# A hybrid decoder layer on one core: decay products and first-level operands of the HGRN2 heads computed in the gate projection

## The chip, the cores and the metric

The kernel runs on one core of one Trainium2 chip. The metric is the device time in microseconds of an execution; the time of a kernel is the median over its runs. Engines are named as in the profile: PE is TensorE, DVE is VectorE, ACT is ScalarE, POOL is GpSimd, SP is SyncE, whose queue issues nearly all loads and stores in program order.

## The reference, cut to what matters

One decoder layer on 1024 tokens with 16 meta tokens ahead of them: an HGRN2 recurrence with four heads beside a causal pooling branch, the two joined by sigmoid gates, then a gated MLP. The change lies in the recurrence and in what feeds it:

```
u = rmsnorm(h, mix_norm_pre[l])
proj = u @ w_in[l]
q, f_logit, i_in, g_out, v_pool, gate_a, gate_b = jnp.split(proj, cuts, axis=-1)
...
f = lb + (1.0 - lb) * jax.nn.sigmoid(fl)
k = (1.0 - lb) * jax.nn.sigmoid(-fl)
...
b = jnp.cumsum(lf, axis=2)
o_inter = jnp.einsum('bhtk,bhkv->bhtv', q * jnp.exp(b), state)
decay = jnp.where(causal, jnp.exp(jnp.where(causal, diff, 0.0)), 0.0)
scores = jnp.einsum('bhtk,bhtsk,bhsk->bhts', q, decay, k)
```

`lf` is the logarithm of `f`, `diff` the difference of two values of `b`. The score of a query at t and a key at s is thus the sum over 128 channels of q times k times the product of all f between s and t. The state carries the same products from chunk to chunk.

## The kernel before, in words

Values are float32, and every matmul operand is split into a high and a low part (`whi`, `wlo`; `uhi`, `ulo`), so that three passes make one product (L304, L305, L307 in the Strassen stages; L204, L205, L208 elsewhere). The stages follow one another: the normed input and the value projection, to about 85 us; the **Strassen pass**, 89.6 to 326 us; the **heads' stage**, 327 to about 584, in which the recurrence shares the engines with the pooling branch; then the mixer and the MLP.

The Strassen pass makes the projections for the forget logits (units F0, F1), the queries (Q0, Q1) and the branch gates (A0 to A3, B0 to B3), in the order F0, Q0, F1, Q1, A0 and on. A unit is 256 columns, that is two heads of F or Q, and takes seven products instead of eight. Each product accumulates in one of four PSUM pairs (`P`). Its weight operand is split four products ahead: ScalarE makes `whi` (L249), VectorE `wlo` (L250). Where the operand is a sum of weight blocks, GpSimd forms it first (`swa`, `swb`; L275 to L278) as soon as the raw weights (`wraw`) have landed. VectorE adds products up: L349 and L358 within a unit, and `put_gate` (L862, L864) for a finished part, which frees the PSUM pair. A part is one head and one half of the tokens.

For a part of an F unit `put_gate` calls `put_f`: ScalarE takes the sigmoids, VectorE scales and floors f (L635, L636), then divides k by f at odd positions for the smallest blocks (L647, L648), giving `kb`. f, k and kb are stored to DRAM (`fscr`, `kscr`, `kbscr`). A part of a Q unit is stored as it is (`qscr`). Temporary tiles come from one pool of 26 slots (`slot`), and a new tile waits until the last use of the slot it takes.

In the heads' stage `ORDER` is a string whose words say which step comes next in the program: `h0` to `h3` advance one head by one step, `PVa0` and the like are halves of the pooling projection (tile `ppv`), `G` the output gate (`pg`), `PP`, `BA`, `BB` the pooling and branch products (`pbb`), `sp` and `sa` elementwise steps, `w` weights for the next stage. Every engine works in its own program order, so an instruction behind a waiting one waits too.

`head_steps` loads f, q, kb and k of a head (L655 to L658), about 0.5 MB each. Causal scores are made in chunks of 128 tokens, by levels of block size 1 (the `sb` product, L719), 2, 4, 8, 16, 32 and 64 (the `sl` products, L696 and L690). At a level the keys of an even block have been multiplied by the f up to their block's end, the queries of an odd block by the f from its start. `grow(lv)` takes operands from one level to the next: keys L673 (`uk`), queries L679 (`uq`; at level 1 it is L677), and the block products of f themselves L681, in place in f. The words in `POOLED` go to GpSimd, among them `uk1` of all heads. Ahead of the `sb` product L714 multiplies the queries at odd positions by f. Scores go from PSUM to SBUF by masked copies (L711, L721) up to level 16 and by plain copies on VectorE at levels 32 and 64 (L705). After the last level k is transposed (`pt`, L748, L751), the states are made (`ds`, L765, with L768 taking the product of f over a chunk as decay), and the output (`po`, L785, L786) is normed by `ms` (L794 to L796) and gated.

## Time and profile before

| | us |
|---|---|
| median of three runs | 1337.79 |
| lowest, highest | 1334.33, 1338.15 |
| the profiled execution itself | 1336.16 |
| its span, first to last instruction | 1334.5 |
| PE busy | 1292.2 |
| DVE busy | 972.5 |
| ACT busy | 519.0 |
| POOL busy | 405.2 |

The granted TensorE clock is 0.988 on average over the span. How such a profile is read: times are microseconds from the first instruction; an engine's idle time is put down to what ended it; idle time of an engine that is not the bottleneck costs nothing. A row of a group gives line, engine, operation, tiles, shapes and count, then busy time, mean nanoseconds of one, and the idle time ahead of it. A row of a timeline gives start, duration, engine and line. A row of waits gives who waited for whom: total, times, longest.

### The profile page before, as it was taken

The numbers are of one execution on the slowest core, as the hardware profiler recorded it, in microseconds if no ns is written. First come the engines' busy times: TensorE is split into PE (matmuls) and PEld (weight loads), VectorE is DVE, ScalarE is ACT, GpSimd is POOL, SyncE is SP. The second block draws the span as 40 slices with busy tenths as digits, with TensorE's granted clock in tenths as the row PEclk, the third lists the DMA queues.
The fourth block names the chain that finished last, engine by engine and source line by source line (L and its number), as shares of the span: only waits on it lengthen the run. The fifth ranks groups of instructions, "written<-read, shape, count | busy, mean of one in ns | idle before, by whom it ended". The sixth has DMA issues, their size and how long they took to land.

```text
span 1334.5 us, 21944 instructions
## 1 busy us (share of the span) xinstructions
PE 1292.2 (97%) x8617; PEld 1143.3 (86%) x8617; DVE 972.5 (73%) x1287; ACT 519.0 (39%) x891; POOL 405.2 (30%) x325
## 2 busy tenths in 40 slices
PE   8999999999789879999999999999999999999997
PEld 6799899999788779987899888888888888888886
DVE  6768965542786976686668999888988885455757
ACT  5554433333125445224664222222222223454543
POOL 3015333322354100052026555446556652000000
PEclk9999999999899889999999999999999999999999
DMA  8135643334232276887686777776767799676644
GB/s 271 41 109 178 199 136 103 111 119 146 92 114 100 65 253 191 305 286 248 225 301 225 209 206 191 201 205 152 180 164 148 178 244 301 216 230 223 221 173 158
DMA packets 143802, 247.62 MB, mean 186 GB/s; under 512 B 11000, under 2 KB 75164, under 8 KB 143698
## 3 DMA queue, kind: packets, MB, share of 16 engines
q1 hardware_dynamic: 131634, 221.83, 49.4%
q0 software_dynamic: 12064, 24.38, 10.9%
q8 instruction: 68, 1.11, 0.3%
q14 instruction: 36, 0.29, 0.1%
HBM read 174.11 MB, written 95.09 MB: 202 GB/s over the span
## 4 chain that ended last, share of the span: by engine, by line
PE 62%; DVE 0%; issue 0%; ACT 0%; DMA 0%; DVEq 0%
PE P L305 11%; PE P L304 11%; PE P L307 11%; PE pd L184 5%; PE pd L185 5%; PE pd L186 5%; PE pm L184 2%; PE pm L185 2%; PE pm L186 2%; PE pba L204 1%; PE pba L205 1%; PE pba L208 1%; PE pbb L204 1%; PE pbb L205 1%; PE pbb L208 1%; PE pt L1271 1%
## 5 line engine op out<-in xcount | busy, mean ns | idle before, releaser
L305 PE MATMUL P<-v,whi 128*128 128x512 f32 (+2 forms) x408 | 140.7, 353 | 0.0
L304 PE MATMUL P<-v,whi 128*128 128x512 f32 (+2 forms) x408 | 140.7, 352 | 0.0
L307 PE MATMUL P<-v,wlo 128*128 128x512 f32 (+2 forms) x424 | 135.1, 349 | 0.0
L275 POOL TENSOR_TENSOR swa<-wraw,wraw 128x512 f32<-128x512 f32 x32 | 48.5, 1516 | 192.1 <-DMA wraw<-in_w_in_dram 98.7
L249 ACT CAST whi<-wraw 128x512 fp32r<-128x512 f32 x90 | 53.1, 618 | 102.3 <-PE P L305 75.7
L1511 DVE TENSOR_TENSOR rot<-wraw,rot 128x1024 fp32r<-128x1024 f32 x31 | 38.0, 1224 | 72.2 <-ACT rot L1510 72.2
L304 PEld LDWEIGHTS P<-v,whi 128*128 128x128 f32 x408 | 76.7, 188 | 10.4
L305 PEld LDWEIGHTS P<-v,whi 128*128 128x128 f32 x408 | 76.6, 188 | 10.2
L307 PEld LDWEIGHTS P<-v,wlo 128*128 128x128 f32 x424 | 74.1, 188 | 10.8
L185 PE MATMUL pd<-rot 128*128 128x512 f32 x272 | 82.1, 389 | 0.0
L186 PE MATMUL pd<-rot 128*128 128x512 f32 x272 | 82.1, 389 | 0.0
L184 PE MATMUL pd<-rot 128*128 128x512 f32 x272 | 81.1, 389 | 0.1
L250 DVE TENSOR_TENSOR wlo<-wraw,whi 128x512 fp32r<-128x512 f32 x86 | 77.4, 922 | 2.7 <-ACT whi L249 2.7
L250 DVE TENSOR_TENSOR wlo<-swb,whi 128x512 fp32r<-128x512 f32 x64 | 67.6, 1064 | 9.7 <-ACT whi L249 9.6
L249 ACT CAST whi<-swa 128x512 fp32r<-128x512 f32 x64 | 38.1, 618 | 92.6 <-PE P L305 77.4
L304 PE MATMUL P<-uhi,whi 128*128 128x258 f32 (+2 forms) x240 | 68.6, 303 | 0.0
L305 PE MATMUL P<-ulo,whi 128*128 128x258 f32 (+2 forms) x240 | 68.4, 303 | 0.0
L1510 ACT CAST rot<-wraw 128x1024 fp32r<-128x1024 f32 x31 | 32.7, 1054 | 90.7 <-PE pd L186 89.4
L249 ACT CAST whi<-swb 128x512 fp32r<-128x512 f32 x64 | 38.1, 618 | 70.9 <-PE P L305 61.5
L304 PE MATMUL P<-t2h,whi 128*128 128x258 f32 (+2 forms) x228 | 65.2, 304 | 0.3 <-DVE sg L864 0.3
L304 PE MATMUL P<-t4h,whi 128*128 128x258 f32 (+2 forms) x228 | 65.5, 304 | 0.0
L305 PE MATMUL P<-t4l,whi 128*128 128x258 f32 (+2 forms) x228 | 65.3, 304 | 0.0
(383 smaller groups left out, 3884.9 us busy)
## 6 DMA issues: line engine op xcount, KB each, us to landing
wraw<-in_w_in_dram SPq DMA_DIRECT2D x36, 512.0 KB, 4.8
yt<-ysum SPq DMA_DIRECT2D x33, 512.0 KB, 5.4
wraw<-in_ffn_w_gate_dram SPq DMA_DIRECT2D x26, 512.0 KB, 5.9
wraw<-in_ffn_w_up_dram SPq DMA_DIRECT2D x22, 512.0 KB, 6.5
wsum<-in_ffn_w_down_dram SPq DMA_DIRECT2D x22, 512.0 KB, 8.5
wraw<-in_w_out_dram SPq DMA_DIRECT2D x18, 512.0 KB, 5.1
ysum<-ys SPq DMA_DIRECT2D x11, 768.0 KB, 5.6
sa<-sscr SPq DMA_DIRECT2D x16, 513.0 KB, 4.4
```

Source lines behind the costliest of these rows:

```text
L184: pe.matmul(ps, ahi, bhi, start=first, stop=False)
L185: pe.matmul(ps, ahi, blo, start=False, stop=False)
L186: pe.matmul(ps, alo, bhi, start=False, stop=last)
L204: pe.matmul(ps[:, :n], whi[:, k, :], xhi, start=(k == 0), stop=False)
L249: act.copy(hi, src)
L250: (pool_e if 4 <= i < 2 * self.early else dve).tensor_tensor(lo, src, rr(hi), ALU.subtract)
L275: pool_e.tensor_tensor(s1, a21, a22, ALU.add)
L304: pe.matmul(d, whi[:, k, :], xh[:, c : c + w], start=(k == 0 and onto is None), stop=False, **go)
L305: pe.matmul(d, whi[:, k, :], xl[:, c : c + w], start=False, stop=False, **go)
L307: pe.matmul(x[:, o : o + w], wlo[:, k, :], xh[:, c : c + w], start=False, stop=(k == 3), **go)
L1510: act.copy(hi, src)
L1511: dve.tensor_tensor(lo, src, rr(hi), ALU.subtract)
```

## The change

In `put_f` the arithmetic of the forget gate's first level is added: the keys at even positions times the next f (`grow(1)` for keys, now L658) and all products of f over blocks of 2, 4, up to 128 tokens (L667, seven instructions, each made from the one before). They lie behind the part in its own tile, widened to 2 x HX, and are stored to a new tensor `tscr`; the store of k comes after the even positions are changed. The halves of a head are stored separately, each with 32 columns of halo, made by ScalarE copies and GpSimd memsets. `put_q` is new: it loads f of the same head and half back from `fscr`, makes the queries for the `sb` product (L678) and for level 2 (L680), and stores both (`qbscr`, `qscr`).

`head_steps` loads five tensors, qb, kb, q, k and tot (L690 to L694). `grow` keeps the key and query products alone (now L717), one line over both halves of the tokens, reading the totals from `tot`; L714, L677 and L681 have no successor in the heads' stage, and `uk1` leaves `POOLED`. A head has one step fewer, and `ORDER` is written anew. The loads of heads 0 and 1 are to be issued after the pass's last weight load (`gates.loaded`) rather than after the last load of any stage so far. The copies of levels 32 and 64 go to ScalarE (L739).

VectorE's program order at the first F part of the pass, before; `sg` is the part being made (later kb), `fk` holds f and k:

```order
L647 RECIPROCAL sg_1102<-fk_1104 128x256
L648 TENSOR_TENSOR sg_1102<-sg_1102,fk_1104 128x256
L862 TENSOR_TENSOR sg_1145<-p_154_1014,P_164_1118 128x514
L250 TENSOR_TENSOR wlo_1185<-swa_1153,whi_1184 128x512 x2
L250 TENSOR_TENSOR wlo_1243<-swb_1154,whi_1242 128x512
L862 TENSOR_TENSOR sg_1246<-p_166_1148,P_175_1217 128x528
```

The same place now:

```order
L656 TENSOR_TENSOR sg_1104<-sg_1104,fk_1106 128x256
L658 TENSOR_TENSOR fk_1106<-fk_1106 128x272
L667 TENSOR_TENSOR sg_1104<-fk_1106 128x272
L667 TENSOR_TENSOR sg_1104<-sg_1104 128x136
L667 TENSOR_TENSOR sg_1104<-sg_1104 128x68
L667 TENSOR_TENSOR sg_1104<-sg_1104 128x34
L667 TENSOR_TENSOR sg_1104<-sg_1104 128x16
L667 TENSOR_TENSOR sg_1104<-sg_1104 128x8
L667 TENSOR_TENSOR sg_1104<-sg_1104 128x4
L891 TENSOR_TENSOR sg_1158<-p_154_1016,P_164_1131 128x514
L678 TENSOR_TENSOR sg_1158<-sg_1158,fq_1160 128x256
L680 TENSOR_TENSOR sg_1158<-sg_1158,fq_1160 128x512
```

Eight instructions of the F part stand between its last one and the next `put_gate` (L862, now L891), and two of the Q part, which read `fq` loaded back from DRAM, ahead of the next `wlo`. Later in the pass the totals of several parts stand mixed with one another and with the adds.

SP's program order at the end of the pass, before:

```order
L147 DMA wraw_3857<-in_w_in_dram 128x8x128
L871 DMA sscr<-sg_3340 128x512
L655 DMA f_3395<-fscr 128x1056
L656 DMA q_3398<-qscr 128x1026
L657 DMA kb_3397<-kbscr 128x1024
L871 DMA sscr<-sg_3369 128x514
L658 DMA k_3396<-kscr 128x1056
```

And now:

```order
L147 DMA wraw_3978<-in_w_in_dram 128x8x128
L898 DMA sscr<-sg_3474 128x512
L690 DMA qb_3530<-qbscr 128x1024
L691 DMA kb_3529<-kbscr 128x1024
L692 DMA q_3532<-qscr 128x1026
L898 DMA sscr<-sg_3503 128x514
L693 DMA k_3531<-kscr 128x1088
L694 DMA tot_3533<-tscr 128x2x538
L690 DMA qb_3542<-qbscr 128x1024
L691 DMA kb_3541<-kbscr 128x1024
```

The first load of head 0 stands behind the same weight load and the same store (`sscr`, the gates of the branches) in both; what is loaded, and in which order, differs.

VectorE's program order at the start of the heads' stage, before; `near` collects the scores of small blocks:

```order
L714 TENSOR_TENSOR q_3398<-q_3398,f_3395 128x512
L677 TENSOR_TENSOR q_3398<-q_3398,f_3395 128x1024
L721 COPY_PREDICATED near_3457<-mbase,sb_3462 128x256
L714 TENSOR_TENSOR q_3408<-q_3408,f_3405 128x512
L681 TENSOR_TENSOR f_3395<-f_3395 128x528
L677 TENSOR_TENSOR q_3408<-q_3408,f_3405 128x1024
L721 COPY_PREDICATED near_3502<-mbase,sb_3507 128x256
L673 TENSOR_TENSOR k_3396<-k_3396,f_3395 128x264x2
L679 TENSOR_TENSOR q_3398<-q_3398,f_3395 128x256x2
```

And now:

```order
L751 COPY_PREDICATED near_3593<-mbase,sb_3597 128x256
L717 TENSOR_TENSOR k_3531<-k_3531,tot_3533 128x272x2
L717 TENSOR_TENSOR q_3532<-q_3532,tot_3533 128x256x2
L745 COPY_PREDICATED near_3593<-mask_145,sl_3631 128x64x2
L751 COPY_PREDICATED near_3716<-mbase,sb_3720 128x256
L745 COPY_PREDICATED near_3716<-mask_145,sl_3754 128x64x2
L717 TENSOR_TENSOR k_3543<-k_3543,tot_3545 128x272x2
```

The five instructions on q and f ahead of the first growth of k are gone. On PE the order is now 42 pooling matmuls, `sb` of head 0, 16 more, its first `sl`, 14 more, then `sb` and the first `sl` of head 1.

The diff, cut to its core:

```diff
@@ -53,10 +53,10 @@
-ORDER = ("h0 h1 PVa0 h0 h1 PVb0 h0 h1 h0 PVa1 h1 h0 sp0 PVb1 h1 h0 h1 PVa2 sp1 h0 h1 PVb2 h0 h1 h2 h0 PVa3 sp2 h1 h0 h1 h3 "
...
+ORDER = ("h0 h1 PVa0 h0 PVb0 h1 h0 PVa1 h1 h0 sp0 PVb1 h1 h0 PVa2 h1 h0 sp1 PVb2 h1 h0 h2 PVa3 h1 h0 sp2 h3 PVb3 h1 h0 h2 Ga2 sp3 h1 h0 h3 h2 "
...
-POOLED = ("uk1.0 uk1.1 uk1.2 uk1.3 wBA2 wBA6 wBA7 wBB2 wPP2 wPV0 wPV1 wPV2 wPV3 wG2 wG3 "
+POOLED = ("wBA2 wBA6 wBA7 wBB2 wPP2 wPV0 wPV1 wPV2 wPV3 wG2 wG3 "
...
@@ -589,6 +589,13 @@
+    HX = M0 + HN
+
+    TOTALS, at_ = {}, 0
+    for lv in (2, 4, 8, 16, 32, 64, 128):
+        TOTALS[lv] = at_
+        at_ += (HX if lv <= NM else HN) // lv
+    NTOT = at_
...
@@ -625,75 +629,105 @@
-    def put_f(m, half, g):
-
-        n = HN if half else HF
-        both = slot(2 * HP, name="fk")
-        f, k = both[:, :n], both[:, HP : HP + n]
-        act.activation(f, g, AF.Sigmoid)
-        act.activation(k, g, AF.Sigmoid, scale=-1.0)
-        dve.tensor_scalar(f, f, oml[:, m : m + 1], lb[:, m : m + 1], ALU.mult, ALU.add)
-        dve.tensor_scalar(f, f, LOG_FLOOR, None, ALU.max)
-        act.activation(k, k, AF.Copy, scale=oml[:, m : m + 1])
-        t0 = NM + (HF if half else 0)
-        for t, d in ((f, fdr), (k, kdr)):
-            nc.sync.dma_start(d[m][:, t0 : t0 + n], t)
-            if not half:
-                nc.sync.dma_start(d[m][:, :NM], t[:, :NM])
-        f2, k2 = (t[:, n - HN :].rearrange("p (b two) -> p b two", two=2) for t in (f, k))
+    def twos(t):
+        return t.rearrange("p (b two) -> p b two", two=2)
+
+    def put_f(m, half, whole, n):
+
+        g, tot = whole[:, :n], whole[:, HX : HX + NTOT]
+        both = slot(2 * HX, name="fk")
+        f, k = both[:, :HX], both[:, HX:]
+        act.activation(f[:, HX - n :], g, AF.Sigmoid)
+        act.activation(k[:, HX - n :], g, AF.Sigmoid, scale=-1.0)
+        dve.tensor_scalar(f[:, HX - n :], f[:, HX - n :], oml[:, m : m + 1], lb[:, m : m + 1], ALU.mult, ALU.add)
+        dve.tensor_scalar(f[:, HX - n :], f[:, HX - n :], LOG_FLOOR, None, ALU.max)
+        act.activation(k[:, HX - n :], k[:, HX - n :], AF.Copy, scale=oml[:, m : m + 1])
+        if half:
+            pool_e.memset(f[:, :M0], 1.0)
+            pool_e.memset(k[:, :M0], 0.0)
+        else:
+            for t, last in ((f, 1.0), (k, 0.0)):
+                act.copy(t[:, :NM], t[:, NM:M0])
+                pool_e.memset(t[:, NM - 1 : NM], last)
+        nc.sync.dma_start(fdr[m][:, half], f[:, M0:])
         kb = g[:, n - HN :]
-        b2 = kb.rearrange("p (b two) -> p b two", two=2)
-        act.copy(b2[:, :, 0], k2[:, :, 0])
-        dve.reciprocal(b2[:, :, 1], f2[:, :, 1])
-        dve.tensor_tensor(b2[:, :, 1], b2[:, :, 1], k2[:, :, 1], ALU.mult)
+        act.copy(twos(kb)[:, :, 0], twos(k[:, M0:])[:, :, 0])
+        dve.reciprocal(twos(kb)[:, :, 1], twos(f[:, M0:])[:, :, 1])
+        dve.tensor_tensor(twos(kb)[:, :, 1], twos(kb)[:, :, 1], twos(k[:, M0:])[:, :, 1], ALU.mult)
         nc.sync.dma_start(kbdr[m][:, half * HN : half * HN + HN], kb)
+        dve.tensor_tensor(twos(k)[:, :, 0], twos(k)[:, :, 0], twos(f)[:, :, 1], ALU.mult)
+        nc.sync.dma_start(kdr[m][:, half], k)
+        src = f
+        for lv in TOTALS:
+            if lv == 2 * NM:
+                src = src[:, M0 // NM :]
+            src = twos(src)
+            w = src.shape[1]
+            dst = tot[:, TOTALS[lv] : TOTALS[lv] + w]
+            dve.tensor_tensor(dst, src[:, :, 0], src[:, :, 1], ALU.mult)
+            src = dst
+        nc.sync.dma_start(tdr[m][:, half], tot)
+
+    def put_q(m, half, whole, n):
+
+        f = slot(HN, name="fq")
+        nc.sync.dma_start(f, fdr[m][:, half])
+        q, q1 = whole[:, n - HN : n], whole[:, HX : HX + HN]
+        if not half:
+            nc.sync.dma_start(qdr[m][:, :HALO], whole[:, :HALO])
+        dve.tensor_tensor(twos(q)[:, :, 1], twos(q)[:, :, 1], twos(f)[:, :, 1], ALU.mult)
+        nc.sync.dma_start(qbdr[m][:, half * HN : half * HN + HN], q)
+        dve.tensor_tensor(twos(q1), twos(q), twos(f)[:, :, :1].to_broadcast([P, HN // 2, 2]), ALU.mult)
+        nc.sync.dma_start(qdr[m][:, HALO + half * HN : HALO + half * HN + HN], q1)
 
     def head_steps(h):
-        f, k, kb, q = slot(NM + L, name="f"), slot(NM + L, name="k"), slot(NM + L, name="kb"), slot(NM + L, name="q")
+        kb, qb, k, qm, tot = (slot(n, name=w) for w, n in (("kb", SEQ), ("qb", SEQ), ("k", 2 * HX), ("q", TQ),
+                                                           ("tot", 2 * HX)))
+        q = qm[:, HALO:]
+        tot = tot.rearrange("p (s t) -> p s t", s=2)[:, :, :NTOT]
         vmeta = small([NM, P], "vmeta", "vmeta", 2)
-        with tc.issue_after(stage["load"].ins):
-            nc.sync.dma_start(f, fdr[h])
-            nc.sync.dma_start(q[:, NM + T0 :], qdr[h])
-            nc.sync.dma_start(kb[:, M0:], kbdr[h])
-            nc.sync.dma_start(k, kdr[h])
+        with tc.issue_after((stage["load"] if h >= 2 else gates.loaded).ins):
+            nc.sync.dma_start(qb, qbdr[h])
+            nc.sync.dma_start(kb, kbdr[h])
+            nc.sync.dma_start(qm, qdr[h])
+            nc.sync.dma_start(k.rearrange("p (s t) -> p s t", s=2), kdr[h])
+            nc.sync.dma_start(tot, tdr[h])
             nc.sync.dma_start(vmeta, vmd[:, h * P : (h + 1) * P])
         yield
-        pool_e.memset(f[:, NM - 1 : NM], 1.0)
-        pool_e.memset(k[:, NM - 1 : NM], 0.0)
         sc, near = slot(NCH * P, name="sc"), small([P, NCH * SB], "near", "near", 2)
         n3 = near.rearrange("p (c t) -> p c t", c=NCH)
         scm = small([NM, HALO], "scm", "scm", 2)
         pool_e.memset(near, 0.0)
         pool_e.memset(sc, 0.0)
 
+        def own(c):
+            t = (c // 4) * HX + M0 + (c % 4) * P
+            return k[:, t : t + P]
+
         def grow(lv):
-            lo = 0 if lv < NM else M0
-            kc, fc, qc, fq_ = blocks(k, lo, lv), blocks(f, lo, lv), blocks(q, M0, lv), blocks(f, M0, lv)
-            n, nq = (NM + L - lo) // (2 * lv), SEQ // (2 * lv)
-            eng(f"uk{lv}.{h}").tensor_tensor(kc[:, :, 0, :], kc[:, :, 0, :], fc[:, :, 1, :1].to_broadcast([P, n, lv]),
-                                             ALU.mult)
-            if lv == 1:
-                q2 = q[:, M0:].rearrange("p (b two) -> p b two", two=2)
-                dve.tensor_tensor(q2, q2, fq_[:, :, 0, :].to_broadcast([P, nq, 2]), ALU.mult)
-            else:
-                eng(f"uq{lv}.{h}").tensor_tensor(qc[:, :, 1, :], qc[:, :, 1, :],
-                                                 fq_[:, :, 0, :1].to_broadcast([P, nq, lv]), ALU.mult)
-            dve.tensor_tensor(fc[:, :, 0, :1], fc[:, :, 0, :1], fc[:, :, 1, :1], ALU.mult)
+            e = M0 if lv >= NM else 0
+            ks = k.rearrange("p (s t) -> p s t", s=2)[:, :, e:]
+            ks = ks.rearrange("p s (b two h) -> p s b two h", two=2, h=lv)[:, :, :, 0]
+            qs = q.rearrange("p (s b two h) -> p s b two h", s=2, two=2, h=lv)[:, :, :, 1]
+            t0, w = TOTALS[lv], (HX if lv <= NM else HN) // lv
+            x = w - HN // lv
+            tk, tq = (tot[:, :, t0 + o : t0 + w].rearrange("p s (b two) -> p s b two", two=2)
+                      for o in (x if e else 0, x))
+            for t, f in ((ks, tk[:, :, :, 1:]), (qs, tq[:, :, :, :1])):
+                dve.tensor_tensor(t, t, f.to_broadcast(list(t.shape)), ALU.mult)
 
...
                     n = 2 * lv * i
-                    dve.tensor_copy(o3[n : n + lv, :, n + lv : n + 2 * lv], p3[n : n + lv])
+                    act.copy(o3[n : n + lv, :, n + lv : n + 2 * lv], p3[n : n + lv])
                 return
...
-        q2, f2 = (t[:, M0:].rearrange("p (b two) -> p b two", two=2) for t in (q, f))
-        dve.tensor_tensor(q2[:, :, 1], q2[:, :, 1], f2[:, :, 1], ALU.mult)
         ps = bank("sb")
-        for c in range(NCH):
-            for n in range(0, P, SB):
-                own = slice(M0 + c * P + n, M0 + c * P + n + SB)
-                pe.matmul(ps[n : n + SB, c * SB : (c + 1) * SB], kb[:, own], q[:, own], start=True, stop=True)
-        grow(1)
+        for t in range(0, SEQ, SB):
+            c, n = t // P, t % P
+            pe.matmul(ps[n : n + SB, c * SB : (c + 1) * SB], kb[:, t : t + SB], qb[:, t : t + SB], start=True, stop=True)
         dve.copy_predicated(n3, mbase.rearrange("p (o t) -> p o t", o=1).to_broadcast([P, NCH, SB]),
                             ps[:, : NCH * SB].rearrange("p (c t) -> p c t", c=NCH))
-        yield
...
@@ -858,17 +885,17 @@
         kind, j = GUNITS[u]
         m, n = 2 * j + i, ghalo(u) + HN
         at = slice(n, n + HN) if h else slice(0, n)
-        g = slot(at.stop - at.start, name="sg")
+        whole = slot(2 * HX, name="sg")
+        n = at.stop - at.start
+        g = whole[:, :n]
         dve.tensor_tensor(g, a, b, ALU.add)
         if c is not None:
             dve.tensor_tensor(g, g, c, ALU.add)
-        if kind == "F":
-            put_f(m, h, g)
+        if kind in "FQ":
+            (put_f if kind == "F" else put_q)(m, h, whole, n)
             return
-        if kind != "Q":
-            act.activation(g, g, AF.Sigmoid)
-        to = dict(Q=qdr, A=sd, B=sd)[kind]
-        nc.sync.dma_start(to[m + (KD if kind == "B" else 0), :, at], g)
+        act.activation(g, g, AF.Sigmoid)
+        nc.sync.dma_start(sd[m + (KD if kind == "B" else 0), :, at], g)

```

37 lines of the change are left out of this document (16 added, 21 removed).

## The prediction

> **What bounds the kernel now.** I read the busy shares first, then the table of stretches (start:end, length, then each engine's busy time, at the end granted TensorE clock, DMA share, GB/s), then whom TensorE waits for.
>
> ```profile
> PE 1292.2 (97%) x8617; PEld 1143.3 (86%) x8617; DVE 972.5 (73%) x1287; ACT 519.0 (39%) x891; POOL 405.2 (30%) x325
> ```
> ```profile
> 120.00:150.00 30.00, 29.74 (x176) 26.24 (x175) 29.69 (x39) 12.32 (x23) 11.73 (x8) 1.00 0.59 190
> 150.00:180.00 30.00, 30.00 (x201) 27.68 (x200) 26.91 (x35) 12.82 (x24) 11.91 (x8) 1.00 0.54 172
> 180.00:210.00 30.00, 30.00 (x197) 27.53 (x196) 16.91 (x24) 11.30 (x20) 11.41 (x8) 1.00 0.35 119
> ...
> 326.00:340.00 14.00, 12.72 (x137) 12.10 (x136) 2.98 (x4) 2.13 (x3) 5.94 (x7) 1.00 0.98 350
> 340.00:360.00 20.00, 13.13 (x425) 12.67 (x426) 17.91 (x22) 2.52 (x5) 6.64 (x4) 0.74 0.07 21
> 360.00:380.00 20.00, 17.22 (x340) 16.56 (x339) 14.86 (x22) 6.55 (x15) 8.09 (x5) 0.91 0.10 29
> ...
> 420.00:440.00 20.00, 13.25 (x315) 12.36 (x314) 15.89 (x15) 14.04 (x18) 6.02 (x4) 0.89 0.10 29
> 440.00:460.00 20.00, 19.59 (x445) 18.14 (x445) 17.12 (x37) 6.02 (x14) 1.37 (x1) 0.94 0.19 55
> 460.00:480.00 20.00, 12.76 (x141) 11.83 (x130) 18.83 (x37) 11.37 (x26) 0.00 (x0) 0.83 0.68 210
> ```
>
> TensorE is the bound over the whole span. The change touches two stages. In the Strassen pass TensorE never rests, but from 120 to 180 VectorE is just as full (29.69 of 30): it is a second bound, hidden only because it keeps pace. In the heads' stage TensorE does rest, and these are its waits there, 326 to 510:
>
> ```profile
> PE sl L696 <- DVE q L677: 5.5, 1, 5.5
> PE ds L765 <- DMA vh<-vscr: 4.2, 1, 4.2
> PE sl L696 <- DVE q L679: 4.0, 4, 2.6
> PE sb L719 <- DVE q L714: 3.7, 1, 3.7
> PE sl L696 <- issue: 3.0, 1, 3.0
> PE po L785 <- ACT rs L796: 2.9, 1, 2.9
> PE pt L748 <- DVE k L673: 1.5, 1, 1.5
> PE pt L751 <- DVE plo L843: 1.5, 1, 1.5
> PE sl L690 <- DVE q L679: 1.4, 1, 1.4
> PE ppv L204 <- DVE sg L862: 0.9, 1, 0.9
> ```
>
> These are 28.6 us, most of it VectorE. A second loss is in the clock column: busy time times the missing clock is 13.13 x 0.26 + 17.22 x 0.09 + 13.25 x 0.11 + 19.59 x 0.06 + 12.76 x 0.17 = 9.8 us. So the stage loses some 38 us, the pass nothing; the change takes VectorE work out of the first and puts it into the second.
>
> **The pass: what is added.** Per forget-gate call (eight): the level-one k product L658 (128x272) and seven totals L667 (272 down to 4 wide). Per query call (eight): L678 (128x256) and L680 (128x512). Ahead of the first add of unit A0 stand 8, 51, 7 and 7 of these. Nearest rows, of today's program:
>
> ```profile
> 165.57 0.42 DVE L648 TENSOR_TENSOR sg<-sg,fk 128x256 f32<-128x256 f32 x1
> ```
> ```profile
> L648 DVE TENSOR_TENSOR sg<-sg,fk 128x256 f32<-128x256 f32 x8 | 7.8, 981 | 0.1
> ```
> ```profile
> L681 DVE TENSOR_TENSOR f<-f 128x132 f32<-128x132 f32 x4 | 1.7, 426 | 0.0
> L681 DVE TENSOR_TENSOR f<-f 128x66 f32<-128x66 f32 x4 | 1.1, 269 | 0.0
> L681 DVE TENSOR_TENSOR f<-f 128x32 f32<-128x32 f32 x4 | 0.9, 213 | 0.0
> L681 DVE TENSOR_TENSOR f<-f 128x16 f32<-128x16 f32 x4 | 0.7, 186 | 0.1
> L681 DVE TENSOR_TENSOR f<-f 128x8 f32<-128x8 f32 x4 | 0.6, 167 | 0.0
> ```
> ```profile
> 375.26 0.68 DVE L679 TENSOR_TENSOR q<-q,f 128x512 f32<-128x512 f32 x1
> ```
>
> L658 and L678 are priced as the undisturbed L648, 0.42; L680 as the undisturbed L679, 0.68. One call's totals: 0.42 + 0.43 + 0.27 + 0.21 + 0.19 + 0.17 + 0.17 = 1.86, times eight, less five late ones (0.9): 14.0. Sum: 8 x 0.42 + 14.0 + 7 x (0.42 + 0.68) = 25.1 us of VectorE. If each of the widest instructions takes the mean of L648, 0.98, instead, it is 8 x 0.98 + 8 x (0.98 + 1.44) - 0.9 + 7 x (0.98 + 0.98) = 40.0. How much is absorbed?
>
> ```profile
> 108.20 1.84 DVE L250 TENSOR_TENSOR wlo<-swa,whi 128x512 fp32r<-128x512 f32 x2 [3.74 <-ACT whi L249]
> ...
> 175.40 0.69 DVE L862 TENSOR_TENSOR sg<-p,P 128x514 f32<-128x514 f32 x1
> 176.01 1.29 DVE L250 TENSOR_TENSOR wlo<-wraw,whi 128x512 fp32r<-128x512 f32 x2
> 178.17 0.69 DVE L349 TENSOR_TENSOR p<-p,P 128x514 f32<-128x514 f32 x1 [0.88 <-PE P L307]
> 180.89 0.69 DVE L862 TENSOR_TENSOR sg<-p,P 128x512 f32<-128x512 f32 x1 [2.03 <-PE P L307]
> ```
>
> VectorE idles 3.7 us before 108.20, which the first totals can fill, and from there to 178 hardly at all. At 178.17 it waits for TensorE again: the 175.40 add is where it has caught up. Products end 2.72 us apart (180.89 - 178.17), and each has one of four PSUM pairs, so an add may come three products late, less its own 0.69, before TensorE stands: 7.5 us. What is left delays TensorE: 25.1 - 3.7 - 7.5 = 13.9, I take **+14**. After that VectorE has 13 us of 30 free (180 to 210) and catches up; TensorE, at 30.00 of 30, does not, so the delay stays. Bounds: +8 if two more products count as slack, since weights are split four products ahead (13.9 - 5.4); +29 from the sum of 40.0 (40.0 - 3.7 - 7.5). I stay by the undisturbed rows, since GpSimd is busy for only 23.6 of these 60 us and today's instructions have already taken their share of that.
>
> That contention is a row of its own:
>
> ```profile
> 128.10 1.78 DVE L250 TENSOR_TENSOR wlo<-wraw,whi 128x512 fp32r<-128x512 f32 x1
> ```
> ```profile
> 127.58 1.74 POOL L276 TENSOR_TENSOR swa<-swa,wraw 128x512 f32<-128x512 f32 x1
> ```
>
> This shape takes 1.78 beside GpSimd's weight sums, and 1.29 for two of it at 176.01, alone. The Trainium skill, GPSIMD Engine Reference, section 1. Specifications, has the rule: GpSimd shares its SBUF interfaces with VectorE, and instructions with two SBUF inputs contend. The trace agrees; all that is added reads two SBUF operands, and were all of it stretched, the sum would be the +29 above: the first rival.
>
> Also added: stores and loads by SP (the totals, the q copies, f read back). DMA is 0.59 busy there; but SP issues in order and GpSimd's sums wait for the weights behind those stores. Priced at nothing while weights arrive early; at 5 if a weight load is late.
>
> **The heads' stage: what goes.** L714, L677 and all L681 leave VectorE, the level-one k product leaves GpSimd, the twelve copies of L705 go to ScalarE, which is at most 14 of 20 busy. What opens in place of the waits at the start, by the landing of loads:
>
> ```profile
> 334.35 0.69 DVE L714 TENSOR_TENSOR q<-q,f 128x512 f32<-128x512 f32 x1 [7.54 <-DMA q<-qscr]
> ...
> 340.63 2.76 DVE L714 TENSOR_TENSOR q<-q,f 128x512 f32<-128x512 f32 x1 [2.60 <-DMA q<-qscr]
> ```
> ```profile
> 327.35 0.32 PE L204 MATMUL ppv<-uhi,whi 128*128 128x346 f32 x1
> 327.51 0.32 PE L205 MATMUL ppv<-ulo,whi 128*128 128x346 f32 x1
> ...
> 343.44 1.08 PE L719 MATMUL sb<-q,kb 128*32 128x32 f32 x64 [3.68 <-DVE q L714]
> ```
>
> The second load landed at 334.3, the sixth at 340.6: 1.6 us each. SP's order keeps head 0's loads behind the same store as before, so "behind its weights" brings nothing here. There are now five loads a head. Head 0's first product needs loads 1 and 2 (334.3), head 1's needs 6 and 7 (342.2), its level one needs load 9 (345.4). Walking the new order from 327.0 (42 pooling matmuls, head 0's first product, 16, its level one, 14, head 1's first product, its level one; 0.16 us a pooling matmul by 327.51 - 327.35, 1.08 a block of head products, as at 343.44), TensorE waits 0.6, 0.9 and 2.1 us: 3.6. Gone from the waits above: 5.5, 4.0, 3.7, 3.0, 1.5 and 1.4, together 19.1. Staying: 4.2 (vh), 2.9, 1.5, 0.9. New waits later, where plo and level products now share VectorE with head 2's growth: 0 to 4, I take 1.5. So the waits change by -19.1 + 3.6 + 1.5 = -14.0; bounds -8 (half of the L679 and k waits remain under GpSimd's adds, 4 new) and -18. The clock, at its worst after the waits of 3.7 and 5.5 that go, gives 6 of 9.8 back (2 to 8): **-20** together, -10 to -26.
>
> A rule for the clock: the Trainium skill, TensorE: Matmul & The Clock Gate, Part 1, section What's actually happening, says an idle window of about 3.4 us halves the clock. By it only the vh wait still costs (12.76 x 0.17 = 2.2) and 7.6 come back, 1.6 more than I take; but 360 to 380 shows 0.91 where the longest wait was 2.6, so not by that alone.
>
> **Sum.** 14 - 20 = -6 against the execution's own 1336.16 (span 1334.5 and 1.66 around it), which lies 1.63 under the median 1337.79. Median: 1337.8 - 6 = about 1331.
>
> **Rivals.** (1) *VectorE cannot carry the pass* (slower): the added instructions are stretched by GpSimd's sums. For: VectorE is at 29.69 of 30, and L648's mean is 0.98. Against: GpSimd has 12 of 30 us. Price +29, gain -20: 1347. It decides once the add of 175.40 comes more than 20 us late by TensorE's clock of products, as the gain is 20. The Trainium skill's rule on shared interfaces speaks for it. Chance 0.2. (2) *A wait takes the place of the removed ones*: the loads of head 1 to 3, five each, or plo become late, so the waits give 8 and the clock 4, for the pass's 14: 1340. For: the DMA share is 0.98 already from 326 to 340; against: from 340 to 380 it is at most 0.10. Chance 0.18. (3) *The pass absorbs it*: both at their good ends, +8 and -26: 1320. For: the order puts adds between the small totals; against: the idle time of 3.7 us is all there is. Chance 0.2.
>
> **How the numbers follow.** Forecast 0.42 (1325 to 1337), rivals 0.2, 0.18, 0.2. A measurement of this kernel tells 0.3%, 4 us, from no change. Faster: 0.34 of the forecast and rival 3: 0.54. Within: 0.08 and most of rival 2: 0.24. Slower: rival 1 and the rest of 2: 0.22. The range takes in most of rivals 1 and 3: 1314 to 1348.
>
> **What would show it.** The last Strassen product ends 8 to 20 us later than 326; VectorE is near 30 of 30 from 110 to past 195, and TensorE's new waits fall between 130 and 200, on sg, p or wlo. Heads: 326 to 510 shrinks by about 20, TensorE waits there fall to about 14, and none names the q products of level one. I am wrong if the pass ends where it did, if it is over 20 late, or if waits on qb, kb, k or tot loads exceed 6 us.

## The result, and the profile after

The changed kernel takes 1342.78 us (median of 7 runs, 1340.48 to 1347.53); the kernel before, measured along with it, 1336.47 (7 runs, 1334.33 to 1338.15). The ratio is 1.0052, 95% interval 1.0036 to 1.0068: slower by half a per cent, 6.3 us. The forecast was 1331, faster; the range, 1314 to 1348, held the time. One execution, the profiled one of run e9 below, ran at a mean clock of 0.654 and took 1821.2 us; its trace is not read.

The profiled execution took 1343.94 us, span 1342.2, so 7.8 over the one shown of before. I place these 7.8 first, by three marks: the first pooling product (`ppv`), where the Strassen pass has ended, the first product of `pm`, where the heads' stage has ended, and the end. The tile views of ppv and pm, of before and of the changed kernel (line, engine, operation, count, shortest/median/longest ns, first and last start, shapes):

```profile
L204 PE MATMUL ppv<-uhi,whi x96: 316/323/657, 327.0 to 401.6; 128*128 128x346 f32 x64, 128*128 128x348 f32 x32
```
```profile
L184 PE MATMUL pm<-whi,zc x128: 389/389/500, 586.7 to 686.0; 128*128 128x512 f32 x128
```
```profile
L204 PE MATMUL ppv<-uhi,whi x96: 317/323/657, 343.3 to 408.5; 128*128 128x346 f32 x64, 128*128 128x348 f32 x32
```
```profile
L184 PE MATMUL pm<-whi,zc x128: 389/389/501, 594.4 to 693.8; 128*128 128x512 f32 x128
```

The pass ends 16.3 us later (343.3 - 327.0; forecast 14). The heads' stage shrinks from 259.7 (586.7 - 327.0) to 251.1 (594.4 - 343.3), by 8.6 where 20 were forecast. The rest, 747.8 in both spans (1334.5 - 586.7, 1342.2 - 594.4), is unchanged. So 16.3 - 8.6 = 7.7, which is the whole difference of the spans.

**The pass.** The table of stretches of the changed kernel, columns as in the prediction:

```profile
120.00:150.00 30.00, 22.62 (x132) 19.48 (x130) 29.44 (x51) 12.57 (x24) 11.25 (x14) 0.99 0.53 179
150.00:180.00 30.00, 27.77 (x143) 24.42 (x144) 27.25 (x53) 10.23 (x20) 11.63 (x13) 0.90 0.60 194
```

VectorE was at 29.69 in the first row before and could not get fuller: it has 51 instructions now instead of 39, and TensorE drops from 29.74 to 22.62. TensorE's waits from 90 to 340 (who, for whom: total, times, longest):

```profile
PE P L304 <- DVE sg L893: 6.9, 2, 6.1
PE P L304 <- DVE sg L891: 2.6, 3, 1.1
PE P L307 <- DVE wlo L250: 1.6, 1, 1.6
PE P L304 <- DVE p L358: 1.2, 1, 1.2
```

These are 12.3 us, all on VectorE (one of 0.3 on ScalarE's `whi` comes to them); before there was one wait of 0.3 in the pass. The second row above also has a clock of 0.90: 27.77 x 0.10 = 2.8 us, which the prediction did not price. It lies at the longest wait, which ends here (timeline of TensorE: start, duration, idle before it):

```profile
150.65 0.57 PE L304 MATMUL P<-t2h,whi 128*128 128x272 f32 x1 [6.11 <-DVE sg L893]
```

From 149.29, inside this wait, the clock is at half for 6.83 us, so the products behind it run slowly too.

**The heads' stage.** TensorE's waits of the changed kernel, 342 to 515:

```profile
PE sl L730 <- issue: 3.8, 2, 3.1
PE ms L821 <- ACT rh L862: 2.8, 1, 2.8
PE sl L730 <- DMA k<-kscr: 1.8, 1, 1.8
PE pt L779 <- ACT sc L739: 1.7, 1, 1.7
PE pt L776 <- DVE plo L870: 1.4, 1, 1.4
PE sl L725 <- DVE q L717: 1.0, 1, 1.0
PE sb L750 <- DMA kb<-kbscr: 1.0, 2, 0.6
```

With three more of 0.9 and one of 0.2 these are 16.4; before, the same list came to 29.8. So the waits fell by 13.4; the forecast was 14.0. The reader is to see that the longest single wait is now 3.1, where 5.5, 4.2 and 3.7 stood before. And yet the clock did not come back:

```profile
340.00:360.00 20.00, 16.75 (x285) 15.51 (x283) 4.23 (x8) 4.31 (x7) 5.61 (x4) 1.00 0.89 319
360.00:380.00 20.00, 18.88 (x463) 18.25 (x464) 9.39 (x16) 3.17 (x6) 3.97 (x4) 0.83 0.04 12
...
420.00:440.00 20.00, 16.90 (x292) 16.32 (x291) 10.82 (x23) 6.80 (x12) 6.57 (x4) 0.90 0.19 56
440.00:460.00 20.00, 15.26 (x319) 13.87 (x319) 11.14 (x20) 16.25 (x26) 1.56 (x1) 0.76 0.27 81
460.00:480.00 20.00, 20.00 (x253) 18.75 (x252) 12.70 (x18) 11.89 (x25) 0.00 (x0) 0.92 0.09 27
480.00:510.00 30.00, 26.92 (x177) 25.80 (x177) 22.00 (x44) 12.72 (x28) 0.00 (x0) 0.94 0.82 263
```

By the prediction's formula: 18.88 x 0.17 + 16.90 x 0.10 + 15.26 x 0.24 + 20.00 x 0.08 + 26.92 x 0.06 = 11.8 us, against 9.8 before. The stage's 8.6 are then -13.4 of waits, +2.0 of clock, +1.3 of a new wait at its end (`pm` for ScalarE's `zc`, at 593.2) and +1.5 that these rows don't assign.

**What the clock follows.** Half clock comes in pieces of 3.41, 6.83 or 10.24 us, one, two or three times 3.41. In the heads' stage of the changed kernel they start at 360.92, 436.01, 453.08 and 483.80 and last 6.83, 6.83, 10.24 and 3.41. That is 27.3 us, and it was 27.3 us before as well (10.24, 3.41, 6.83 and 6.83, from 343.33, 370.64, 435.50 and 473.04). What changed is how much of it TensorE was busy: 19.6 us before, 25.2 now. A busy microsecond at half clock loses half, so the loss goes from 9.8 to 12.6. Taken by these pieces the clock is +2.8 and not +2.0; with a wait of 0.5 behind 515 that leaves 0.2 of the 1.5 unassigned.

The starts, too, lie whole multiples of 3.41 apart (75.09, 17.07 and 30.72 are 22, 5 and 9 of them). So the clock looks set on a fixed grid of windows of 3.41 us. These are the windows right ahead of the four pieces:

```profile
357.51:360.92 3.41, 1.23 (x120) 1.15 (x123) 0.44 (x1) 1.36 (x4) 3.02 (x2) 1.00 0.73 273
432.60:436.01 3.41, 0.48 (x57) 0.39 (x47) 1.90 (x4) 3.16 (x5) 1.18 (x1) 1.00 0.57 167
449.67:453.08 3.41, 0.58 (x2) 0.30 (x2) 2.22 (x2) 3.40 (x7) 1.04 (x1) 1.00 0.00 0
480.39:483.80 3.41, 0.66 (x5) 0.42 (x6) 3.41 (x7) 3.41 (x9) 0.00 (x0) 1.00 0.43 96
```

TensorE was busy for 0.48 to 1.23 of 3.41 us in them, but none is idle throughout. In the last one the waits of 1.4 and 1.7 on `pt` from the list above stand one behind the other. In the first, TensorE issued 120 matmul instructions, more than in the twice as long piece behind it (111); but they are small, 32 wide by 32 or 16 columns, and the longest wait among them is 1.8 us. The theory that the runs below test: half clock follows a window of about 3.4 us in which the array did little, **whether it waited or had small products**. Its rival: only the time counts in which TensorE waited, added up over the window. The Trainium skill, TensorE: Matmul & The Clock Gate, Part 1, section What's actually happening, ties half clock to an idle window of about 3.4 us; the lengths agree (3.41 and its multiples), while here a window in which TensorE was busy for 1.23 of 3.41 us counted as idle.

### The profile page after: what moved, and what is told of

It reads as the page before. It is cut to its first block, busy times and chain, and to the rows that moved or that the text cites. A ratio compares the mean times of both kernels' runs of the same rounds, so it can differ in the third digit from the quotient of the medians.

```text
span 1342.2 us, 22057 instructions
## 1 busy us (share of the span) xinstructions
PE 1299.6 (97%) x8617; PEld 1147.9 (86%) x8617; DVE 969.0 (72%) x1319; ACT 525.2 (39%) x911; POOL 397.4 (30%) x329
## 4 chain that ended last, share of the span: by engine, by line
PE 55%; DVE 0%; ACT 0%; DVEq 0%; issue 0%
PE P L305 11%; PE P L304 11%; PE P L307 11%; PE pd L184 5%; PE pd L186 5%; PE pd L185 5%; PE pm L184 2%; PE pm L186 2%; PE pm L185 2%; PE pt L1298 1%; PE pm L1353 1%; DVE hrow L1708 0%; ACT junk L1695 0%; DVE acc L1771 0%; DVE p L1474 0%; DVEq L1799 0%
## 5 line engine op out<-in xcount | busy, mean ns | idle before, releaser
L275 POOL TENSOR_TENSOR swa<-wraw,wraw 128x512 f32<-128x512 f32 x32 | 53.3, 1665 | 170.6 <-DMA wraw<-in_ffn_w_gate_dram 72.0
L305 PEld LDWEIGHTS P<-v,whi 128*128 128x128 f32 x408 | 76.6, 188 | 10.2
L250 DVE TENSOR_TENSOR wlo<-wraw,whi 128x512 fp32r<-128x512 f32 x86 | 73.6, 877 | 2.7 <-ACT whi L249 2.7
L250 DVE TENSOR_TENSOR wlo<-swb,whi 128x512 fp32r<-128x512 f32 x64 | 64.1, 1008 | 8.4 <-ACT whi L249 8.4
L305 PE MATMUL P<-t2l,whi 128*128 128x258 f32 (+2 forms) x228 | 66.2, 308 | 0.0
```

The source lines that it names most:

```text
L250: (pool_e if 4 <= i < 2 * self.early else dve).tensor_tensor(lo, src, rr(hi), ALU.subtract)
L275: pool_e.tensor_tensor(s1, a21, a22, ALU.add)
L305: pe.matmul(d, whi[:, k, :], xl[:, c : c + w], start=False, stop=False, **go)
```

## The experiments

My theory of the pass: VectorE's added instructions among the F and Q units are the whole delay. The rival: the new stores and loads on SP make weights late. My theory of the heads: the clock, as above. Rivals: ScalarE's moved copies, and that clock is lost only where TensorE waits anyway. Line numbers are those of each kernel. All ratios are to the kernel before, run on the same chip. Differences from the changed kernel are of medians from different chips; by the ratios they come out up to 2 us larger or smaller.

**1 and 2. The added VectorE work moved behind A0.** Kernel e1_late_fq stores f, k and q raw, and does the level-one products and totals one task per store in units A0 to A3, from tiles loaded back; e2_late_f does so for the F part alone.

```diff
+        nc.sync.dma_start(krd[m][:, half], k)
...
+        late.append(lambda: late_f(m, half))
+
+    late = []
+
+    def late_f(m, half):
...
+        nc.sync.dma_start(f, fdr[m][:, half])
+        nc.sync.dma_start(k, krd[m][:, half])
         dve.tensor_tensor(twos(k)[:, :, 0], twos(k)[:, :, 0], twos(f)[:, :, 1], ALU.mult)
...
+        nc.sync.dma_start(qrd[m][:, half], whole[:, n - HN : n])
+        late.append(lambda: late_q(m, half))
...
         act.activation(g, g, AF.Sigmoid)
+        if late:
+            late.pop(0)()
```

> All added VectorE work (L658, the totals, the two query products) is taken out of the F and Q units: f, k and q are stored raw, loaded back and worked on in the puts of units A0 to B1, where VectorE has some 14 us of 30 free. Theory (VectorE's load in the F/Q units delays the pass by 16.3 us, the clock eats the heads' gain): the last Strassen product ends within 4 us of 326, the heads keep their 10 us, so about 1328, 8 us below the kernel before. Rival (the delay comes from SP's longer queue and slot waits, not from VectorE): more loads and stores make it no better, pass end 338 or later, 1339 or more.

> Only the F part is put off (L658 and totals, about 17 of 25 us); the query products stay in the Q units with their load of f. Theory by VectorE's load: 25.1 less 17.4 leaves 7.7, under the 11.2 that can be absorbed: pass end within 4 us of 326, about 1329. Rival (the query part, which waits for f from DRAM in the middle of VectorE's queue, is what costs): pass end 334 or later, 1335 or more.

Measured: e1 1335.40, ratio 0.9986 (0.9973 to 0.9998); e2 1335.87, 0.9987 (0.9977 to 0.9998). Both are faster than the changed kernel by some 7 us and hardly faster than before. Unit A0's products start at 169.25 before, at 184.20 in the changed kernel (+15.0), at 170.02 in e1 (+0.8) and at 172.84 in e2 (+3.6). So F's part made 11.4 of the 15 and Q's 2.8, and VectorE's added work there, with its waits for `fq`, is the cause; e1 has more stores and loads than the changed kernel, and with them the weights came in time, which speaks against SP's queue as the cause of this delay. But the pass of e1 still ends at 338.8, 11.9 late, where the theory had 4 at most, and that of e2 at 337.9. VectorE's waits in e1, 180 to 300:

```profile
DVE ql L695 <- DMA ql<-qrscr: 8.4, 5, 3.0
DVE tl L679 <- DMA fl<-fscr: 6.8, 4, 2.6
DVE ql L695 <- issue: 4.0, 1, 4.0
```

VectorE stood 19.2 us at the late tasks, 15.2 of it for tiles that were not back yet, with the adds that free PSUM queued behind; TensorE waited 9.5 us for VectorE from 170 on. The work, moved to where VectorE had room, brought the stall of its loads with it. So only 4.5 of e1's gain over the changed kernel lie in the pass. Another 5.9 lie in the heads' stage (245.2, 584.0 - 338.8), whose code is the same: there half clock came to 17.1 us instead of 27.3.

**5. The same with the loads two stores earlier.** Kernel e5_late_pre issues each task's loads two stores ahead of its work. It also spreads the tasks over 24 stores instead of 16.

```diff
+        if begun and begun[0][0] <= puts[0] - 2:
+            begun.pop(0)[1]()
+        if late and puts[0] % 3:
+            begun.append((puts[0], late.pop(0)()))
```

> As the version with all added VectorE work put off to units A and B, but each task's loads are issued two puts ahead of its arithmetic and the tasks are spread over 24 puts instead of 16. There TensorE lost 9.6 us in units A1 to A3 while VectorE stood 21 us waiting for the loads of f, k and q. Theory (VectorE has the time, the late loads cost it): pass end within 4 us of 326, about 1327. Rival (SP's queue, full of weight loads and stores, makes loads late however early they are asked for): pass end 334 or later, 1334 or more.

Measured: 1334.62, ratio 0.9977 (0.9965 to 0.9989). The pass ends at 335.9, 8.9 late. VectorE's waits, 180 to 338:

```profile
DVE ql L708 <- DMA ql<-qrscr: 13.2, 5, 4.7
DVE fl L680 <- DMA fl<-krscr: 9.3, 4, 3.0
```

22.5 us still, and pass end and time are where the rival on this run had them. SP issues in order, and its queue stood for 35.6 us, from 170 to 335, at the gates' stores (L929), which waited for ScalarE's `sg`; an earlier place in the program does not pass what stands ahead. The loads on another queue were not tried.

**3. The copies back on VectorE.** Kernel e3_copies_dve undoes this one part.

```diff
-                    act.copy(o3[n : n + lv, :, n + lv : n + 2 * lv], p3[n : n + lv])
+                    dve.tensor_copy(o3[n : n + lv, :, n + lv : n + 2 * lv], p3[n : n + lv])
```

> The changed kernel with the copies of levels 32 and 64 back on VectorE. Theory: they are off the chain, 1343 give or take 2. Rival (ScalarE's later releases make the waits of 1.7 and 3.1 us that TensorE now has on ScalarE in the heads' stage): 3 or more us faster, 1339 or less.

Measured: 1339.76, ratio 1.0026 (1.0012 to 1.0039): some 3 us under the changed kernel by the medians, though the two intervals touch. That is between the theory (1341 to 1345) and its rival (1339 and less). The wait of 1.7 for ScalarE's `sc` is gone, and that of `pm` falls from 1.3 to 0.7; but one of 2.4 (`pt` for ScalarE's `kt`) is new, all waits of the stage come to 18.0 where the changed kernel has 18.2, and half clock lies where it did. So it is not shown that the copies belong to the loss.

**4. Filler products in the short windows.** Kernel e4_fill issues 54 full transposes, whose results are overwritten, in the windows ahead of the pieces of half clock, and computes the same.

```diff
+FILL = {(1, "sb"): 6, (0, 2): 4, (1, 2): 14, (0, 4): 6, (1, "ms"): 24}
+    def fill(ps, n):
+        for _ in range(n):
+            pe.transpose(ps[:, :P], ident, ident)
...
             ps = bank("sl")
+            fill(ps, FILL.get((h, lv), 0))
```

> The changed kernel with 54 filler transposes of 0.11 us (6 us if none were hidden) ahead of head 0's and 1's first level products and of head 1's norm sum, inside waits; they write PSUM that the real product then overwrites. Theory (the clock halves after a 3.41 us stretch in which little of the array works, waits and small products alike): the half-clock episodes near 361 and 453, 17 us at half clock, go or shorten; 8 us won, 2 to 3 lost to fillers that don't fit: 1336 to 1339. Rival (an episode comes from something else, such as the wait alone or the small products themselves): episodes stay, time 1343 to 1348.

Measured: 1334.52, ratio 0.998 (0.9968 to 0.9991): 8.3 us under the changed kernel and below the theory's 1336, by adding work to the busiest engine. Its fillers, and its stretches:

```profile
L603 PE MATMUL sl<-ident 128*128 128x128 f32 x24 | 3.4, 280 | 0.0
L603 PE MATMUL ms<-ident 128*128 128x128 f32 x24 | 2.8, 273 | 0.0
L603 PE MATMUL sb<-ident 128*128 128x128 f32 x6 | 0.8, 273 | 0.0
```
```profile
360.00:380.00 20.00, 18.52 (x479) 17.54 (x478) 10.13 (x16) 3.17 (x6) 5.14 (x4) 1.00 0.03 8
...
420.00:440.00 20.00, 20.00 (x446) 19.13 (x445) 13.26 (x26) 10.13 (x18) 6.77 (x4) 1.00 0.27 82
```

The clock is 1.00 from 360 to 380 and 420 to 440, where it was 0.83 and 0.90. The pass ends at 342.6, much as in the changed kernel; the heads' stage takes 242.6 (585.2 - 342.6) instead of 251.1. Half clock comes to 10.2 us there, 27.3 before. The fillers' 7.0 us of TensorE are covered by waits and by the clock. This run cannot tell the theory from its rival: full products fill the waits, too.

**7. The same places, small products.** Kernel e7_fill_small has 189 products, 32 wide by 16 columns, there instead.

```diff
+    def fill(ps, n):
+        for _ in range(n * 7 // 2):
+            pe.matmul(ps[:SB, : SB // 2], ident[:, :SB], ident[:, : SB // 2], start=True, stop=True)
```

> The changed kernel with fillers at the same places and of about the same total busy time, but made of 189 products of 32 x 32 by 16 instead of 54 transposes of 128 x 128 by 128. Theory (the clock counts how much of the array works, so small products count as idle): the half-clock episodes near 361 and 453 stay, 1341 to 1346. Rival (being busy at all keeps the clock): they go, 1334 to 1338.

Measured: 1345.21, ratio 1.0061 (1.0045 to 1.0076). The time lies in the theory's range, but the trace speaks against the theory. Two stretches in which small products stand without a break, and the 3.9 us ahead of the first piece of half clock in the heads (6.83 from 354.45):

```profile
455.70:461.20 5.50, 5.50 (x170) 5.44 (x169) 3.59 (x5) 5.49 (x11) 1.56 (x1) 1.00 0.01 3
362.50:367.90 5.40, 5.40 (x204) 5.19 (x204) 0.45 (x1) 2.09 (x4) 4.05 (x2) 1.00 0.06 15
```
```profile
350.50:354.40 3.90, 1.43 (x87) 1.26 (x83) 0.36 (x1) 0.00 (x0) 0.00 (x0) 1.00 1.04 413
```

The first row is nearly all fillers, 168 instructions (each small product shows as two); it holds a whole window, 456.85 to 460.26, with nothing else in it. TensorE is busy throughout, and the clock stays at 1.00 there and until 487. The second row, fillers and the equally small products of head 1, keeps it until 443. Half clock follows the third row, in which TensorE was busy for 1.43 of 3.9 us: it waited 1.55 for `k`, and then 2.0 for what the profile does not name. So **it is not the size of the products that counts here, but the time TensorE stands still**. The rival is right on the clock: half clock fell to 17.1 us (6.83, 6.83 and 3.41). The kernel is slow for another reason: the small fillers take 12.8 us of TensorE against 7.0, and cover fewer of the waits.

The traces of all kernels here but e9, laid on the grid from 20 to 1300 us, say the same. The 48 windows right ahead of half clock have TensorE busy for 0 to 1.85 us; the others at full clock, some 4370, for 1.63 or more. So the edge lies at about half of the window. Whether size counts at the edge, where both kinds lie, stays open.

**8. Fillers in the kernel before.** Kernel e8_before_fill puts 106 transposes into the long waits of the kernel before.

```diff
+FILL = {(1, "sb"): 22, (0, 2): 16, (1, 2): 6, (3, 2): 36, (2, "ds"): 26}
```

> The kernel before with 106 fillers of 0.11 us inside its own waits: head 1's first product (3.7 us), head 0's and 1's level 2 (3.0), head 3's level 2 (5.5), head 2's states (4.2). Theory (the half-clock time after these waits, 27 us, is a cost of its own and fillers prevent it): 7 to 11 us below the kernel before, with the waits themselves unchanged. Rival (the clock falls whatever is put there, or fillers delay the real products): no more than 3 us below it, or slower.

Measured: 1340.22, ratio 1.0023 (1.0012 to 1.0034), slower. Half clock in the heads fell from 27.3 to 13.6 us, yet the stage took 261.8 (589.2 - 327.4), 2.1 more. The wait that carries it:

```profile
PE sl L702 <- DVE q L684: 9.3, 4, 4.6
```

This wait was 4.0 before (the row of L679 in the prediction); the one of 5.5 for L677 fell to 1.4 in return, and those of 3.7 and 4.2 went or shrank. TensorE reached VectorE's operands earlier in part, and waited there instead. One account fits all filler runs. The fillers' own time is added, the waits that they cover are taken off, and so is half of TensorE's busy time at half clock (profiled executions, us):

| | fillers | waits of the stage | half clock | half of the busy time in it | stage |
|---|---|---|---|---|---|
| before | 0 | 29.8 | 27.3 | 9.8 | 259.7 |
| e8: before, 106 transposes | 13.6 | 21.9 | 13.6 | 6.8 | 261.8 |
| changed | 0 | 18.2 | 27.3 | 12.6 | 251.1 |
| e4: changed, 54 transposes | 7.0 | 10.7 | 10.2 | 4.6 | 242.6 |
| e7: changed, 189 small products | 12.8 | 14.1 | 17.1 | 7.2 | 254.3 |

The sums give +2.7 for e8 (13.6 - 7.9 - 3.0), -8.5 for e4 (7.0 - 7.5 - 8.0) and +3.3 for e7 (12.8 - 4.1 - 5.4); measured are +2.1, -8.5 and +3.2. So e8 won 3.0 at the clock, where its theory had 7 to 11, and its fillers cost more than they covered.

**6, 9, 10, 11. Toward a better version.** Kernel e6_late_pre_fill is e5 with e4's fillers and e3's copies. e9_tot_pool leaves all in the F unit but computes the totals (L667) on GpSimd:

```diff
-            dve.tensor_tensor(dst, src[:, :, 0], src[:, :, 1], ALU.mult)
+            pool_e.tensor_tensor(dst, src[:, :, 0], src[:, :, 1], ALU.mult)
```

e10_tot_pool_fill is e9 with fillers and copies, e11_fill_dve the changed kernel with these two alone.

> The same with the 54 filler transposes ahead of level products and the norm sum, and the copies of levels 32 and 64 on VectorE. Theory (the three effects are separate: 8 us by fillers, 3 by the copies): about 10 below the kernel without them. Rival (fillers hide in waits that the earlier pass end moves, so that half-clock episodes come back): less than 4 below it.

> The changed kernel with the 56 totals (L667, 14 us of VectorE) on GpSimd, where the F and Q units leave 18 us of 30 free. Theory (VectorE's load delays the F and Q units): unit A0 starts within 4 us of the kernel before's 169.25 instead of 15 late, pass end 330 to 334, 1332 to 1335. Rival (GpSimd's totals stand ahead of its weight sums and stretch VectorE's instructions): A0 8 us late or more, 1338 or more.

> The same with the 54 filler transposes and the copies of levels 32 and 64 on VectorE. Theory (separate effects): 8 to 11 below the version without them, 1323 to 1327, the fastest here. Rival (effects overlap): 1329 or more.

> The changed kernel, totals on VectorE as it has them, with the fillers and the copies of levels 32 and 64 on VectorE. Theory (the copies cost 3 by themselves, the fillers 8): 1331 to 1333. Rival (both mend the same episode): 1334 to 1336, as the fillers alone.

Measured: e6 1329.30, 0.9947 (0.9932 to 0.9961); e9 1331.69, 0.9956 (0.9942 to 0.9969); e10 **1327.03**, 0.9925 (0.9900 to 0.9951); e11 1333.69, 0.9989 (0.9967 to 1.0010). So e10 beats the changed kernel by 16 us and the one before by 10. The fillers and copies together gave 5.3 on e5 and 4.7 on e9, about half of what their theories had. The stretches of e10:

```profile
120.00:150.00 30.00, 27.26 (x160) 24.61 (x159) 30.00 (x40) 11.85 (x23) 26.20 (x40) 0.94 0.69 232
150.00:180.00 30.00, 26.76 (x166) 23.83 (x165) 29.97 (x43) 13.10 (x25) 20.20 (x35) 1.00 0.74 247
```

A0 starts at 173.05 (+3.8) and the pass ends at 334.4 (+7.4): half of the delay is gone. But VectorE, without the totals, is at 30.00 and 29.97 of 30: GpSimd is at 26.20 instead of 11.25, and a part of what was taken off VectorE comes back in its other instructions: 21.9 us of totals left it, and its busy time in the pass fell by 10.2, from 170.83 to 160.66. e11 against e4 says nothing on the copies beside fillers: its interval holds e4's time.

## Why the prediction was wrong

**The bound.** Right: VectorE is the second bound of the pass from 120 to 180, and what was added there came out as TensorE's waits on sg, p and wlo, 9.6 of the 12.3 us between 130 and 200, 2.7 already ahead of 130.

**The pass, +14.** 16.3 was measured: 12.3 of waits, 2.8 of clock, 1.2 unassigned. The result is near, but the terms under it were off and cancelled. VectorE's groups of the whole pass, 90 to 342, those that the change added (the six small totals in one row) and four that were there, of the changed kernel (busy us, mean ns | idle before):

```profile
L250 DVE TENSOR_TENSOR wlo<-swa,whi 128x512 fp32r<-128x512 f32 x24 | 21.0, 892 | 0.6 <-ACT whi L249 0.6
L250 DVE TENSOR_TENSOR wlo<-wraw,whi 128x512 fp32r<-128x512 f32 x28 | 20.1, 740 | 0.0
L250 DVE TENSOR_TENSOR wlo<-swb,whi 128x512 fp32r<-128x512 f32 x24 | 17.0, 723 | 8.4 <-ACT whi L249 8.4
L667 DVE TENSOR_TENSOR sg<-sg 128x136 f32<-128x136 f32 (+5 forms) x48 | 16.1, 353 | 0.4
...
L680 DVE TENSOR_TENSOR sg<-sg,fq 128x512 f32<-128x512 f32 x8 | 6.5, 817 | 0.1
L658 DVE TENSOR_TENSOR fk<-fk 128x272 f32<-128x272 f32 x8 | 6.1, 762 | 0.0
L667 DVE TENSOR_TENSOR sg<-fk 128x272 f32<-128x272 f32 x8 | 5.8, 726 | 0.0
...
L678 DVE TENSOR_TENSOR sg<-sg,fq 128x256 f32<-128x256 f32 x8 | 4.5, 560 | 3.6 <-DMA fq<-fscr 3.6
...
L656 DVE TENSOR_TENSOR sg<-sg,fk 128x256 f32<-128x256 f32 x8 | 4.1, 508 | 0.2
```

The added ones (L667 twice, L680, L658, L678) sum to 16.1 + 5.8 + 6.5 + 6.1 + 4.5 = 39.0 us by their rows, not 25.1: close to the stretched bound of 40.0, the work of the first rival. But the older instructions got shorter in return. Of before:

```profile
L250 DVE TENSOR_TENSOR wlo<-swa,whi 128x512 fp32r<-128x512 f32 x24 | 24.2, 1023 | 3.9 <-ACT whi L249 3.7
L250 DVE TENSOR_TENSOR wlo<-wraw,whi 128x512 fp32r<-128x512 f32 x28 | 22.3, 819 | 0.0
L250 DVE TENSOR_TENSOR wlo<-swb,whi 128x512 fp32r<-128x512 f32 x24 | 18.6, 791 | 9.6 <-ACT whi L249 9.6
```

L250 fell from 65.1 to 58.1, and L656 (L648 before, 7.8 in all) to 4.1, so 10.7 came back. And the records of neighbouring instructions overlap, so that sums of rows come out too large. VectorE's busy time in the pass, the third of the busy times, of before and of the changed kernel:

```profile
90.00:326.00 236.00, 235.74 (x1583) 218.14 (x1581) 146.13 (x200) 91.33 (x169) 79.07 (x54) 1.00 0.41 134
```
```profile
90.00:342.00 252.00, 239.49 (x1581) 220.48 (x1580) 170.83 (x280) 92.77 (x176) 82.89 (x70) 0.99 0.46 150
```

It grew by 24.7 us, close to my 25.1 for the calls ahead of A0 and below the 27.0 that the same prices give for all of them. So the sum held, by luck: the added instructions cost more than their undisturbed rows, and the older ones less than before. The stretching seems to follow GpSimd's busy time, whichever VectorE instruction stands beside it: that time hardly grew (79.07 to 82.89). e10 bears this out. With GpSimd busy for 105.75 us of the pass, the same L250 took 64.8 again and L656 7.2. What I had put at nothing is the waits for the loads of fq, 3.6. With them VectorE was pushed by 28.3 and the pass by 16.3, so 12.0 were absorbed, where I counted 11.2. The first rival's time, 1347, is nearer to the result than mine. The add of 175.40, by which it was to be decided, comes at 198.05, 22.7 late on VectorE; but TensorE's products come 15.0 late at A0 and 16.3 at the end, and never 20.

**New loads.** Right in size: the waits for head 0 and 1 at the start, forecast 3.6, are 1.8, 1.0 and 0.7 (the shorter of the two of "issue"), 3.5. None of the waits names level one's q products.

**Waits of the heads, -14.0.** Right in the sum, -13.4, and that by luck, since the members are other ones. The vh wait of 4.2, which was to stay, went too; new, where I had 1.5, are 3.1 at 433 (the longer of the two of "issue"; by the order of events perhaps a PSUM bank that ScalarE's sigmoid still held), 2.8 for its `rh` and 1.7 for its copies.

**The failed step: the clock, "at its worst after the waits of 3.7 and 5.5 that go, gives 6 of 9.8 back".** By the same slices it took 2.0 more, a miss of 8.0 out of the 11.4 between the forecast of -20 and the -8.6 measured (the others: 0.6 of waits, 1.3 of `pm`, 1.5 unassigned there). I took half clock for the price of the longest waits, and let it go with them. I had a row that spoke against it, and quoted it: 360 to 380 at 0.91 with a longest wait of 2.6. Half clock follows windows of 3.41 us in which TensorE stands still for more than about half, in one wait or in several. In the changed kernel other waits, of 3.1, 2.8, 1.8, and 1.7 beside 1.4, leave four windows as empty as the long ones did. So 27.3 us of half clock stayed, and since waits had gone from these 27.3 us, TensorE was busy in 25.2 of them instead of 19.6: the price rose. Fillers in the empty windows took it back down, to 10.2 us with full products (e4) and to 17.1 with small ones (e7); e4's were worth 8.3 us, e7's cost more than they brought. With that term at +2 in place of -6, the forecast is 14 - 14 + 2 = +2, about 1340.

**Open.** Where exactly between 1.63 and 1.85 us of busy time a window turns, and whether size counts there; what the copies are worth; the 1.2 us unassigned in the pass.

## What to carry to other kernels

Where the granted clock is below 1.00, add up how long TensorE was busy in the 3.41 us ahead of each piece of half clock; several waits of one to two microseconds empty a window as a long one does. Taking out the longest waits brings no clock back if others leave as many windows empty, and it makes TensorE busier in the slow time that stays. A few products put into such windows can be worth more than they cost: weigh their own time against the waits that they cover and half of the busy time at half clock. Work that is moved onto an engine at 29.7 of 30 comes out on the bound less what the queues absorb (16.3 of 28.3 us here); moving it later in the program, or to GpSimd, gave back only a part. Price a stretch by contention once for the stage, not instruction by instruction: what the new instructions suffered, the old ones were spared.

## What the runs showed of the hardware

- Half clock came in pieces of 3.41, 6.83 and 10.24 us in every trace read here, on a grid of 3.41 us. In the window ahead TensorE was busy for 0 to 1.85 us; one of them holds 120 small matmul instructions (the changed kernel, 1.23 us).
- 168 instructions of 32 wide by 16 columns, back to back for 5.5 us, kept the clock at 1.00 (e7).
- 54 transposes of 128x128, 7.0 us of TensorE, made the kernel 8.3 us faster; 106 of them, 13.6 us, in the kernel before, made it 3.4 slower.
- Added VectorE rows of 39.0 us came with 10.7 us less in rows that were there already: L656 takes 0.51 in the mean, 0.98 before. With GpSimd busy for 105.75 us of the pass instead of 82.89 (e10), it took 0.89.
- In e5, where SP issued the loads two stores earlier, VectorE still waited 13.2 and 9.3 us for them in all.
